# A branch for the middle expert: 64 or 128 places, chosen by its count of tokens

## The chip, the cores and the metric

The kernel runs on one core of a Trainium2 chip. The metric is the device time of one execution, in microseconds. A profiled execution also gives a trace: each instruction of the engines TensorE (PE, its weight loads PEld), VectorE (DVE), ScalarE (ACT) and GpSimd (POOL), and the DMA issues of SyncE (SP).

## What is computed

A diffusion block of two layers in float32 on 256 latent and 256 context tokens of width 1024. Layer 0 has differential attention and a SwiGLU network. Layer 1 has a recurrent mixer (RG-LRU) and, for the latent tokens, a mixture of eight experts, two for each token. The change lies in these experts, the last stage before the final norm:

```python
def swiglu(h, w_gate_up, w_down):
    gate, up = jnp.split(h @ w_gate_up, 2, axis=-1)
    return (jax.nn.silu(gate) * up) @ w_down

def moe_swiglu(h, router_w, w_gate_up, w_down):
    logits = (h @ router_w).astype(jnp.float32)
    top_val, top_idx = lax.top_k(logits, TOP_K)
    top_w = jax.nn.softmax(top_val, axis=-1)
    gates = ...
    for e in range(N_EXPERTS):
        y = y + gates[..., e:e + 1] * swiglu(h, w_gate_up[e], w_down[e])
    return y
```

An expert's inner width is 3584, so its weights are 1024 x 7168 and 3584 x 1024, and the eight together are 352 MB.

## The kernel before

Each expert computes only the tokens that chose it. They are gathered by a matmul with a one-hot matrix into columns, its "places", and scattered back the same way. Expert number 0 comes first; the other seven come in falling order of their counts of tokens, which the kernel finds itself (`by_counts`, L1643); SyncE then loads the seven experts' numbers into registers (`load_numbers`, L1915) and reads their weights from addresses made of them. An expert is "wide" (128 places) or "small" (64 places); `SMALL` (L46) makes the last three by count small, the other five wide. Should a count exceed the places, a test at the end (L1926 to L1928) runs the whole stage again for the tokens left over.

An expert's inner width is cut into seven chunks of 512. A chunk has a gate-up product (`gate_up`, L1727; four weight tiles), the activation, transposes of it (`act_T`, L1757) and a down product (`down`, L1776; two weight tiles), so six tiles of 1 MB. A tile is 128 x 2048 float32. A wide product needs its weights as two parts, high and low: ScalarE writes the high part (L135), VectorE the low one (L139), in halves of a tile, up to six halves ahead of the matmuls (`HL`), and each pair of weights and tokens takes three matmuls (L265 to L267), 48 for a gate-up product and 24 for a down one. A small product takes the tile as it is, in full float32: two matmuls of 64 columns stand beside each other in the array (L1738, L1784), and none of its weights are split.

A stream (`class stream`, L168) loads the tiles in the order of use into 13 places in SBUF. A place comes free when a wide tile's second half has been split, or when a small product has ended with it (`next_two`, L219); SyncE issues the next load then. `ORDER` (L46 to L56) sets the chunks' order: seven wide ones of expert 0, then seven groups of "small, wide, small, wide, small, wide, wide". `products` (L230) puts the down products behind: the down product of a small chunk comes just ahead of the next small gate-up, that of a wide chunk after the next wide gate-up.

Around a new expert, `experts` (L1704) works so: the one-hot matrix (`who`) is made after the gate-up product two chunks ahead; the gather's matmuls (`gather_mm`, L1310) come before the gate-up product of the chunk ahead, and the gathered tokens are scaled, shifted and split (`gather_split`, L1318) after it. In the middle of a wide gate-up product (`between`, L1891) stand the transposes and at most one scatter of an expert that is done. On the engines PE, DVE, ACT and POOL the order is as it is written; SyncE's is the framework's. The last chunk of all belongs to a wide expert: its end scatters, adds, squares, takes the root of the norm and writes the output (`scale_out`, L1806; `final_out`, L1698).

Of the kernel before, what the change touches and what calls it, by code (L numbers as in the profile page):

```python
# [45 lines left out]
SMALL = (5, 6, 7)  # L46
PLACES = tuple(64 if i in SMALL else P for i in range(NE))


_S = [(i, c) for i in SMALL for c in range(EC)]  # L50
_W = [(i, c) for i in range(NE) if i not in SMALL for c in range(EC)]
ORDER = _W[:EC]
for _n in range(EC):
    _s, _w = _S[3 * _n:3 * _n + 3], _W[EC + 4 * _n:EC + 4 * _n + 4]
    ORDER += [_s[0], _w[0], _s[1], _w[1], _s[2], _w[2], _w[3]]

# [32 lines left out]
def body(tc, nc, cst, rope, vec, lamv, modb, fing, x, ctx, w_m0, w_mod, w_q, w_k, w_v, w_o,  # L89
# [25 lines left out]

    def bank(name):
        return psp.tile([P, 512], F32, name=name, tag="b")
# [15 lines left out]
    def split_hi(h):  # L133
        h["hi"] = hip.tile([P, 1024], F32R, name="whi", tag="whi")
        A.copy(h["hi"][:, :h["w"]], h["src"])  # L135

    def split_lo(h, eng=V):
        h["lo"] = hip.tile([P, 1024], F32R, name="wlo", tag="wlo")
        eng.tensor_tensor(h["lo"][:, :h["w"]], h["src"], h["hi"][:, :h["w"]].bitcast(F32), op=OP.subtract)  # L139
# [18 lines left out]

    class part_of:
# [8 lines left out]
    class stream:  # L168
# [3 lines left out]
        def __init__(self, aps):  # L172
            self.aps, self.free, self.loaded, self.halves = aps, [], [], []
            self.n_split = self.n_used = self.n_tile = 0
            self.ahead, self.until = HL, len(aps)

# [53 lines left out]
    def products(order, small):  # L230
# [3 lines left out]
        for n, (i, c) in enumerate(order):  # L234
            s = i in small
            if s and pend[s]:
                yield "dn", *pend[s]
            yield "gu", i, c
            if not s and pend[s]:
                yield "dn", *pend[s]  # L240
            pend[s] = i, c
            if not s and pend[True] and not any(j in small for j, _ in order[n:]):
                yield "dn", *pend[True]
                pend[True] = None
        yield "dn", *pend[False]
# [1051 lines left out]
    def gather_banks(n, w=P):  # L1297

        per = KD // n
        banks = [bank("gath") for _ in range(n)]  # L1300
        return [(banks[k // per][:, k % per * w:(k % per + 1) * w], k % per, banks[k // per]) for k in range(KD)]
# [8 lines left out]
    def gather_mm(oh, small):  # L1310

        gps = gather_banks(1, 64) if small else gather_banks(2)
# [5 lines left out]
    def gather_split(eb, gps, scalar=(0, 1, 2, 3)):  # L1318

        hts = [eb.tile([P, 4, P], F32, name="ght", tag=tag) for tag in ("yh", "yl")]  # L1320
        xH = eb.tile([P, KD, P], F32R, name="xH", bufs=1)
        xL = eb.tile([P, KD, P], F32R, name="xL", bufs=1)

        def scaled(hb):
            for k in range(4 * hb, 4 * hb + 4):
                ht, g_, s_ = hts[hb][:, k % 4], gs2[:, k:k + 1], sh2[:, k:k + 1]
                if k in scalar:
                    A.activation(ht, gps[k][0], AF.Identity, scale=g_, bias=s_)  # L1328
                else:
                    V.tensor_scalar(ht, gps[k][0], g_, s_, op0=OP.mult, op1=OP.add)  # L1330

        scaled(0)
        if len(scalar) == 4 and scalar[3] == 3:
            scaled(1)
        for hb in range(2):
            ks = slice(4 * hb, 4 * hb + 4)
            A.copy(xH[:, ks], hts[hb])  # L1337
            V.tensor_sub(xL[:, ks], hts[hb], xH[:, ks].bitcast(F32))  # L1338
            if hb == 0 and scalar[3] != 3:
                scaled(1)  # L1340
        return xH, xL

    def gather_whole(eb, gps):

        ps = gps[0][2].rearrange("p (k n) -> p k n", k=KD)
        xF = eb.tile([P, KD, 64], F32, name="xF", bufs=1)
# [4 lines left out]
    with tc.manual_schedule(engines={ENG.PE, ENG.DVE, ENG.Activation, ENG.Pool, ENG.SP}):  # L1351
# [129 lines left out]
        first = stream(expert_tiles(ORDER, SMALL, numbers.__getitem__))  # L1481
        first.until = EC * 6 - 2
        first.add([rawp] * RAW)
# [6 lines left out]
        first.add(mrawL[:3])  # L1490
# [14 lines left out]
        first.add([part_of(mrawH[0][:, j]) for j in range(2)])  # L1505
        first.add(mrawL[3:])
# [12 lines left out]
        cnt = mo.tile([P, 1], I32, name="cnt")  # L1519
# [68 lines left out]
        first.add([part_of(mrawH[1][:, j]) for j in range(2)])  # L1588
# [26 lines left out]
        first.add(mrawR)  # L1615
        eb = pool(name="eb0", bufs=2)
# [5 lines left out]
        def gates_of_tokens():  # L1622

            scr = eb.tile([P, 74], F32, name="scr", tag="yh")
# [18 lines left out]
        def by_counts():  # L1643

            ck = bank("ck")
            mm(ck[:, 0:NE], ones, mask[:, 0], start=True, stop=False)
            mm(ck[:, 0:NE], ones, mask[:, 1], start=False, stop=True)
            scr = eb.tile([P, 3, NE * NE], F32, name="scr", tag="yl")
# [3 lines left out]
            V.tensor_copy(row[:, 0], ck[:, 0:NE])  # L1652
            V.tensor_add(row[:, 1], row[:, 0], lead)
# [15 lines left out]
            pick(row[:, 1], row[:, 0])  # L1669
            V.tensor_sub(row[:, 1], row[:, 1], places)  # L1670
# [3 lines left out]
            V.tensor_copy(cnt, cm)  # L1674
# [10 lines left out]
    def square(t, dh):  # L1685

        junk = bank("junk")
        A.activation(junk, XL[:, t, dh * 512:dh * 512 + 512], AF.Square, scale=D ** -0.5, accum_out=ssf[t][:, dh:dh + 1])
        if dh == 0:
            G.tensor_tensor(late["fo"][:, t, 0:512], XL[:, t, 0:512], late["fg"][:, 0:512], op=OP.mult)  # L1690
# [7 lines left out]
    def final_out(t):  # L1698
        rs, fo = ssf[t][:, 0:1], late["fo"][:, t]
# [4 lines left out]
    def experts(half, eb, E, tiles, order, small):  # L1704


        last, queue = order[-1][0], []

        def who(i, again=False):
            oh = eb.tile([P, 2, P], F32, name="ohp", bufs=1) if again else hp.tile([P, 2, P], F32, name="oh", tag="cr")  # L1710
            return one_hot(oh, key_at, i, i in small)

        def place(i):

            oh = E[i]["oh"]
            tp = bank("ohT")
            gp = bank("gateps")
# [3 lines left out]
            ohT = eb.tile([P, 2, P], F32R, name="ohTs", bufs=1) if i in small else hp.tile([P, 2, P], F32R, name="ohT", tag="SC")  # L1721
            A.copy(ohT.rearrange("p t n -> p (t n)"), tp[:, 0:2 * P])
            gs_ = eb.tile([P, 1], F32, name="gslot")
            V.tensor_copy(gs_, gp[:, 0:1])
            E[i].update(ohT=ohT, gate=gs_)

        def gate_up(i, c, between):  # L1727
            n = 256 if i in small else 512
            sg = None
            if i in small:  # L1730
                between()
                xF = E[i]["x"]
                gu = [bank("mg")]
# [299 lines left out]
```

## Time and profile before

| | us |
|---|---|
| median of three runs | 1746.3 (1746.25 to 1746.3) |
| profiled execution | 1744.36 |
| its span, first to last instruction | 1742.5 |
| TensorE busy in the span | 1689.8 |
| moved by DMA | 480.31 MB, 276 GB/s over the span |

The profile's page gives busy times of the engines over the span and in 40 slices; the trace behind it answers by line, by stretch of time, by waits, and by the chain of work that ended last. An L with a number is a line of the kernel before. The busy time of a group is the union of its instructions' times; matmuls overlap, so what one takes is read from the chain, in which each piece lasts until the next begins.

### The profile page before, as it was taken

To read this page: it belongs to the slowest core of one execution; us is meant where nothing else is said; L and a number is where in the kernel's file an instruction comes from. 1 tells how busy PE (TensorE), PEld (TensorE's weight loads), DVE (VectorE), ACT (ScalarE), POOL (GpSimd) and SP (SyncE) were. 2 spreads that over 40 slices of the span, in tenths; PEclk is the share of its full clock that TensorE was granted. 3 is DMA by queue.
4 is the path that set the end of the run, shared out by engine and by line. 5 is a ranking of instruction groups with operands and counts; after the bars stand their busy time and mean duration, and the time that the engine had idled before them with its cause. 6 is when DMAs were issued, how large, how long until landed. Compare 5 with 4: busy or idle time off the path is not lost. (4 is left out here: it accounts for less than half of the span.)

```text
span 1742.5 us, 21960 instructions
## 1 busy us (share of the span) xinstructions
PE 1689.8 (97%) x8060; PEld 1233.3 (71%) x8060; DVE 1205.9 (69%) x1694; ACT 885.6 (51%) x1289; POOL 63.4 (4%) x62
## 2 busy tenths in 40 slices
PE   8999999999999999987999999999999999999997
PEld 6877788887788877745786665666665766657564
DVE  5488878777757447897996775576664757648565
ACT  4367664322222216983875654454553645546353
POOL 0011100000000001131000000000000000000000
PEclk9999999999999999998999999999999999999998
DMA  9233323555656413356898899998999999999991
GB/s 375 103 145 146 146 97 118 203 200 193 231 190 238 136 70 121 112 224 241 312 392 308 329 421 405 420 371 355 397 402 420 370 421 391 372 383 411 386 422 50
DMA packets 75484, 480.31 MB, mean 276 GB/s; under 512 B 14284, under 2 KB 14924, under 8 KB 18920
## 3 DMA queue, kind: packets, MB, share of 16 engines
q1 hardware_dynamic: 66976, 474.38, 68.6%
q10 hardware_dynamic: 8392, 4.45, 1.0%
q8 instruction: 65, 1.06, 0.3%
q14 instruction: 51, 0.42, 0.1%
HBM read 477.70 MB, written 1.10 MB: 275 GB/s over the span
## 5 line engine op out<-in xcount | busy, mean ns | idle before, releaser
L139 DVE TENSOR_TENSOR wlo<-raw,whi 128x1024 fp32r<-128x1024 f32 x407 | 484.7, 1217 | 133.8 <-ACT whi L135 132.7
L135 ACT CAST whi<-raw 128x1024 fp32r<-128x1024 f32 x412 | 420.8, 1045 | 244.5 <-PE mg L266 80.2
L265 PE MATMUL mg<-whi,xH 128*128 128x512 f32 x560 | 228.3, 408 | 7.2 <-ACT xH L1337 7.2
L267 PE MATMUL mg<-wlo,xH 128*128 128x512 f32 x560 | 223.5, 399 | 2.0 <-DVE wlo L139 2.0
L266 PE MATMUL mg<-whi,xL 128*128 128x512 f32 x560 | 224.0, 400 | 0.9 <-DVE xL L1338 0.9
L139 DVE TENSOR_TENSOR wlo<-mraw,whi 128x1024 fp32r<-128x1024 f32 x124 | 148.3, 1222 | 35.6 <-ACT whi L135 35.3
L135 ACT CAST whi<-mraw 128x1024 fp32r<-128x1024 f32 x124 | 127.7, 1050 | 46.1 <-PE mg L266 40.6
L265 PE MATMUL gu<-hH,whi 128*128 128x512 f32 (+1 forms) x384 | 143.0, 372 | 0.0
L267 PE MATMUL gu<-hL,whi 128*128 128x512 f32 (+1 forms) x384 | 142.6, 371 | 0.0
L266 PE MATMUL gu<-hH,wlo 128*128 128x512 f32 (+1 forms) x384 | 142.6, 371 | 0.0
L265 PEld LDWEIGHTS mg<-whi,xH 128*128 128x128 f32 x560 | 106.6, 190 | 46.6 <-issue 13.6
L1738 PE MATMUL mg<-raw,xF 128*64 128x512 f32 x464 | 131.1, 594 | 0.0
L267 PEld LDWEIGHTS mg<-wlo,xH 128*128 128x128 f32 x560 | 106.5, 190 | 28.3 <-DVE wlo L139 2.4
L266 PEld LDWEIGHTS mg<-whi,xL 128*128 128x128 f32 x560 | 106.6, 190 | 25.9 <-DVE xL L1338 2.2
L1753 ACT ACTIVATE sges<-mg 128x256 f32<-128x256 f32 x21 | 8.1, 385 | 200.1 <-PE mg L1738 200.1
L265 PE MATMUL yp<-whi,aH 128*128 128x512 f32 x272 | 108.0, 397 | 0.0
L266 PE MATMUL yp<-whi,aL 128*128 128x512 f32 x272 | 107.4, 395 | 0.0
L267 PE MATMUL yp<-wlo,aH 128*128 128x512 f32 x272 | 107.3, 395 | 0.0
L1039 DVE SCALAR_TENSOR_TENSOR mac<-raw,SC,mac 128x512 f32<-128x512 f32 x140 | 98.2, 749 | 3.6 <-DMA raw<-w_mod 2.7
L1754 DVE TENSOR_TENSOR sges<-sges,mg 128x256 f32<-128x256 f32 x21 | 8.9, 422 | 125.4 <-ACT sges L1753 125.4
L1738 PEld LDWEIGHTS mg<-raw,xF 128*64 128x64 f32 x464 | 40.6, 137 | 62.0 <-issue 60.5
L265 PEld LDWEIGHTS gu<-hH,whi 128*128 128x128 f32 x384 | 72.3, 188 | 15.0 <-issue 2.5
(351 smaller groups left out, 3006.1 us busy)
## 6 DMA issues: line engine op xcount, KB each, us to landing
raw<-m_gu SPq DMA_DIRECT2D x158, 1024.0 KB
raw<-m_dn SPq DMA_DIRECT2D x75, 1024.0 KB
mraw<-m_gu SPq DMA_DIRECT2D x66, 1024.0 KB
raw<-w_mod SPq DMA_DIRECT2D x40, 1024.0 KB
mraw<-m_dn SPq DMA_DIRECT2D x37, 1024.0 KB
raw<-w_gu SPq DMA_DIRECT2D x22, 1024.0 KB
mw<-w_m SPq DMA_DIRECT2D x8, 1024.0 KB
raw<-w_dn SPq DMA_DIRECT2D x8, 1024.0 KB
```

What stands on the lines that cost most here:

```text
L135: A.copy(h["hi"][:, :h["w"]], h["src"])
L139: eng.tensor_tensor(h["lo"][:, :h["w"]], h["src"], h["hi"][:, :h["w"]].bitcast(F32), op=OP.subtract)
L265: mm(ps, lh, rh, start=start, stop=False)
L266: mm(ps, ll, rh, start=False, stop=False)
L267: mm(ps, lh, rl, start=False, stop=stop)
L1039: V.scalar_tensor_tensor(ac[:, q], w[:, j], SC[:, k, m:m + 1], ac[:, q], op0=OP.mult, op1=OP.add)
L1738: mm(gu[0][64 * h:64 * h + 64], xF[:, kk], w, start=(kk == 0), stop=(kk == KD - 1), tile_position=(0, 64 * h), skip_group_check=True)
L1753: A.activation(part, ps[:, 0:256], AF.Silu)
L1754: V.tensor_mul(part, part, ps[:, 256:512])
```

## The change

`FLEX = 4` names the expert that is fourth of the seven by count. `by_counts` also writes that expert's count into `cnt`. The stage runs as before up to the third chunk of expert 0 (`BEFORE = 3`); then all engines load the count, and a branch takes one of two bodies. Under 65 tokens, the fourth expert is small too: five wide chunks of expert 0 lead, then come 23 pairs "small, wide" and five small chunks. Otherwise the order is the old one. Each body goes on from copies (`fork`) of the state reached: stream, turns of the tiles, free banks, chunks under way. The loads before the branch are limited to the 28 tiles that both orders share.

So that both bodies can be written from one state, the stage's SBUF tiles and PSUM banks are no longer asked of pools: `ring` gives fixed tiles in turn, `banks` keeps a list of free banks, taken in front and given back behind. With two small chunks in a row, `products` puts the down product of the first behind the second's gate-up, and `between` stands in the middle of that gate-up. Where the new expert is of the other kind than the one before it, `gather` ends before the gate-up product that stands in between, and the one-hot is made in `between`, half a chunk or more earlier. A small expert can now be the last; its scatter goes to four banks. The test for left-over tokens at the end stays.

```diff
-SMALL = (5, 6, 7)
+FLEX = 4
+SMALL = tuple(range(FLEX + 1, NE))
...
+BEFORE = 3
...
+ORDERS = {False: (_mixed(SMALL, EC, "swswsww" * EC), SMALL)}
+ORDERS[True] = _mixed((FLEX,) + SMALL, EC - 2, "sw" * 23 + "s" * 5), (FLEX,) + SMALL
...
+        def fork(self, aps):
+
+            t = stream(aps)
+            t.free, t.loaded, t.halves = list(self.free), list(self.loaded), list(self.halves)
+            t.n_split, t.n_used, t.n_tile = self.n_split, self.n_used, self.n_tile
+            return t
...
-        first.until = EC * 6 - 2
+        first.until = (EC - 2) * 6 - 2
...
+            V.tensor_copy(cnt[:, 1:2], row[:, 1, FLEX:FLEX + 1])
...
             if ahead is not None:
                 gps = gather_mm(E[ahead]["oh"], ahead in small)
+                if (ahead in small) != (i in small):
+                    gather(ahead, gps)
...
                 if c == EC - 3:
                     E[i]["oh"] = who(i, True)
+                if n + 2 < len(order) and order[n + 2][1] == 0:
+                    j = order[n + 2][0]
+                    E[j] = {"oh": who(j)}
...
+                        for t in range(2 if i == last else 0):
+                            sp[t, dh] = pb.take()
+                            mm(sp[t, dh], E[i]["ohT"][rows, t].bitcast(F32), yg[rows], start=True, stop=True,
+                               tile_position=(64 * dh, 0))
...
+                    if last in small:
+                        act_T(*steps[order[-1]])
...
+    with manual():
+        state = experts(eb, E, first, *ORDERS[False], until=BEFORE, numbers_due=True)
...
+    def branch(flex):
+        with manual():
+            t = first.fork(expert_tiles(*ORDERS[flex], numbers.__getitem__))
+            t.load()
+            steps, queue, n, m = state
+            mem.update({k: v.fork() for k, v in before.items()})
+            experts(mem["eb"], {i: dict(e) for i, e in E.items()}, t, *ORDERS[flex], state=(dict(steps), list(queue), n, m))
+
+    fits = nc.values_load(cnt[0:1, 1:2], min_val=0, max_val=SEQ,
+                          skip_runtime_bounds_check_because="a count of at most 256 tokens")
+    with tc.If(fits < 65) as few:
+        branch(True)
+    with few.Else():
+        branch(False)
```

## Rows read from the trace of the kernel before

**Rows 1.** The page's busy times: engine, us, share of the span, instructions.

```profile
PE 1689.8 (97%) x8060; PEld 1233.3 (71%) x8060; DVE 1205.9 (69%) x1694; ACT 885.6 (51%) x1289; POOL 63.4 (4%) x62
```

**Rows 2.** Stretches: length, busy us by engine (instructions), granted clock, DMA share, GB/s.

```profile
900.00:1700.00 800.00, 785.43 (x3574) 519.51 (x3574) 518.93 (x577) 420.04 (x519) 0.00 (x0) 0.99 0.95 387
1000.00:1100.00 100.00, 100.00 (x454) 64.62 (x453) 64.48 (x70) 53.03 (x65) 0.00 (x0) 1.00 1.01 414
1060.00:1080.00 20.00, 20.00 (x96) 14.96 (x96) 16.08 (x21) 14.03 (x18) 0.00 (x0) 1.00 1.01 422
1300.00:1400.00 100.00, 97.88 (x445) 62.74 (x444) 61.65 (x72) 51.04 (x65) 0.00 (x0) 0.98 0.97 399
```

**Rows 3.** SyncE's waits before a load: releaser, us in total, times, longest.

```profile
SPq L122 <- DVE wlo L139: 691.6, 167, 20.0
SPq L122 <- PE yp L1784: 185.2, 20, 10.0
```

**Rows 4.** The chain that ended last, in order of time: start, us, work.

```profile
1669.38 3.58 PE yp L1784 x16
1672.96 6.87 PE mg L1738 x32
1679.83 0.44 PE mg L265
...
1685.63 0.65 PE aT L1761 x6
...
1697.48 3.58 PE yp L1784 x16
```

**Rows 5.** The page's DMA issues: tile, count, size of one.

```profile
raw<-m_gu SPq DMA_DIRECT2D x158, 1024.0 KB
```

**Rows 6.** TensorE's groups: busy us, mean ns, idle us before them and its releaser.

```profile
L265 PE MATMUL mg<-whi,xH 128*128 128x512 f32 x560 | 228.3, 408 | 7.2 <-ACT xH L1337 7.2
...
L1307 PE MATMUL gath<-oh,XN 128*128 128x128 f32 x160 | 19.0, 277 | 1.3 <-DVE oh L1284 1.3
...
L1307 PE MATMUL gath<-oh,XN 128*128 128x64 f32 x96 | 13.2, 304 | 2.4 <-DVE oh L1290 2.4
...
L1761 PE MATMUL aT<-cs,sges 128*128 128x128 f32 x42 | 8.1, 274 | 2.3 <-DVE aL L1773 2.3
```

**Rows 7.** Stretches as in rows 2, just after such waits.

```profile
955.00:960.00 5.00, 5.00 (x17) 3.94 (x16) 1.87 (x2) 2.39 (x3) 0.00 (x0) 0.68 1.01 426
1175.00:1180.00 5.00, 5.00 (x19) 4.42 (x19) 0.00 (x0) 0.21 (x1) 0.00 (x0) 0.50 1.01 428
1350.00:1355.00 5.00, 5.00 (x16) 3.94 (x15) 2.17 (x3) 2.10 (x3) 0.00 (x0) 0.66 1.01 421
1545.00:1550.00 5.00, 4.91 (x14) 3.87 (x15) 1.86 (x3) 1.77 (x2) 0.00 (x0) 0.66 1.01 421
```

**Rows 8.** The test at the end: ns min/median/max, first and last start.

```profile
L1926 PEldq TENSOR_LOAD <-cnt x1: 490/490/490, 1728.1 to 1728.1; - x1
...
L1926 ACTq TENSOR_LOAD <-cnt x1: 1059/1059/1059, 1734.3 to 1734.3; - x1
...
L1928 PEldq COMPARE_BRANCH  x1: 3370/3370/3370, 1728.7 to 1728.7; - x1
...
L1928 ACTq COMPARE_BRANCH  x1: 50/50/50, 1735.4 to 1735.4; - x1
...
L1928 ACTq EVENT_SEMAPHORE  x1: 17/17/17, 1739.4 to 1739.4; - x1
```

**Rows 9.** The end: a piece of the chain, and groups by line as in rows 6.

```profile
1727.24 2.84 PE scat L1853 x6
...
L1764 ACT COPY aF<-aT 128x256 f32<-128x256 f32 x21 | 7.9, 377 | 1.9 <-PE aT L1761 1.9
...
L1790 DVE SCALAR_TENSOR_TENSOR ygs<-yp,gslot,G2b 64x512 f32<-64x512 f32 x6 | 4.5, 750 | 6.6 <-PE yp L1784 6.6
...
L1841 PE MATMUL scat<-ygs,ohTs 64*128 64x512 f32 x24 | 9.0, 637 | 0.9 <-DVE ygs L1790 0.9
```

More of the change, by code (lines that the diff above doesn't have):

```diff
@@ L1480, in body, with places @@
         numbers = {0: 0}
-        first = stream(expert_tiles(ORDER, SMALL, numbers.__getitem__))
-        first.until = EC * 6 - 2
-        first.add([rawp] * RAW)
+        all_places = []
+        def places(pools):
+            new = [part_of(p.tile([P, 2048], F32, name="raw", tag="raw")) for p in pools]
+            all_places.extend(new)
+            return new
+        first = stream(expert_tiles(*ORDERS[False], numbers.__getitem__))
+        first.until = (EC - 2) * 6 - 2
+        first.add(places([rawp] * RAW))
         ws = {}
@@ L1504, in body @@
         mrawH = [hp.tile([P, 2, 2048], F32, name="mraw", tag="hH")]
-        first.add([part_of(mrawH[0][:, j]) for j in range(2)])
-        first.add(mrawL[3:])
+        first.add(places([part_of(mrawH[0][:, j]) for j in range(2)]))
+        first.add(places(mrawL[3:]))
+        halves = ring()
+        for tag in ("whi", "wlo"):
+            halves.put(tag, [hip.tile([P, 1024], F32R, name=tag, tag=tag) for _ in range(HL)])
+        mem["hi"] = halves
         for eng in (G, V, G):
@@ L1587, in body @@
         mrawH.append(hp.tile([P, 2, 2048], F32, name="mraw", tag="hL"))
-        first.add([part_of(mrawH[1][:, j]) for j in range(2)])
+        first.add(places([part_of(mrawH[1][:, j]) for j in range(2)]))
         close(lr2)
@@ L1702, in final_out, with experts @@
         nc.sync.dma_start(out[:, t], fo)
-    def experts(half, eb, E, tiles, order, small):
-        last, queue = order[-1][0], []
+    def experts(eb, E, tiles, order, small, state=None, until=None, numbers_due=False):
+        last, pb = order[-1][0], mem["ps"]
+        steps, queue, n, m0 = state or ({}, [], -1, 0)
         def who(i, again=False):
-            oh = eb.tile([P, 2, P], F32, name="ohp", bufs=1) if again else hp.tile([P, 2, P], F32, name="oh", tag="cr")
+            oh = eb.tile([P, 2, P], F32, name="ohp" if again else "oh")
             return one_hot(oh, key_at, i, i in small)
@@ L1730, in gate_up @@
             if i in small:
-                between()
+                run = order.index((i, c)) and order[order.index((i, c)) - 1][0] in small
+                if not run:
+                    between()
                 xF = E[i]["x"]
-                gu = [bank("mg")]
+                gu = [pb.take()]
                 for kh in range(2):
@@ L1739, in gate_up @@
                                tile_position=(0, 64 * h), skip_group_check=True)
+                    if run and kh == 0:
+                        between()
             else:
                 xH, xL = E[i]["x"]
-                gu = [bank(f"mg{h}") for h in range(2)]
+                gu = [pb.take() for h in range(2)]
                 for kh in range(2):
@@ L1863, in experts @@
             gather(0, gather_mm(E[0]["oh"], 0 in small))
-        todo, n, steps = list(products(order, small)), -1, {}
-        for m, (what, i, c) in enumerate(todo):
+        todo = list(products(order, small))
+        for m in range(m0, len(todo)):
+            what, i, c = todo[m]
+            if what == "gu" and n + 1 == until:
+                return steps, queue, n, m
             if what == "dn":
-                if m == len(todo) - 1 and half == 0:
-                    late["fg"] = mrawR[0].tile([P, D], F32, name="fg", tag="raw")
-                    late["fo"] = mrawR[1].tile([P, 2, D], F32, name="fo", tag="raw")
+                end = m == len(todo) - 1
+                if end:
+                    late["fg"], fo = [tiles.free.pop(0).tile() for _ in range(2)]
+                    late["fg"], late["fo"] = late["fg"][:, 0:D], [fo[:, t * D:(t + 1) * D] for t in range(2)]
                     nc.sync.dma_start(late["fg"], fing.to_broadcast([P, D]))
-                if m == len(todo) - 2:
+                    while queue:
+                        scatter(*queue.pop(0))
+                    if last in small:
+                        act_T(*steps[order[-1]])
+                if m == len(todo) - 2 and last not in small:
                     cur = steps[order[-1]]
```

223 lines of the change are left out of this document (143 added, 80 removed).

## The prediction, made before the change was run

> **What bounds the kernel now.** I read the page's busy times first: TensorE is busy 97% of the span, VectorE 69% [rows 1], so matmuls set the time unless a stage says otherwise. The stage of the change is the experts', about 800 to 1730 us, and it needs a table of its own, by stretches: over 900 to 1700 us TensorE is busy 785 of 800 us, VectorE 519, ScalarE 420, and the DMA engines' share is 0.95 at 387 GB/s [rows 2]. Two things are therefore nearly full, TensorE and the stream of weight tiles. To see which one holds the other, compare stretches: 1060 to 1080 us moves 422 GB/s at a share of 1.01, which I take for the stream's ceiling, while 1300 to 1400 us moves 399 with TensorE at 98% [rows 2]. The stream has holes where TensorE has none worth the name, and the longest waits of the issuing queue are for places that a product still holds (20 waits on the small `yp` products alone, 185.2 us) [rows 3]. So TensorE leads and the stream follows, some 8% below its ceiling (387 against 422).
>
> The chain that ended last then gives prices. A small chunk is its down product, 3.58 us, and its gate-up product, 6.87 us: 10.45 us. A wide chunk runs from 1679.83 to the next small product at 1697.48: 17.65 us, with 0.65 us of transposes of both kinds in it, so 17.0 us of its own [rows 4]. The reference, worked out on its inputs, gives the experts 110 tokens (number 0) and, sorted, 82, 70, 58, 56, 54, 52 and 30: the fourth of seven has 56, not over 64, so the branch with four small experts runs. The margin is 8 tokens.
>
> **The change part by part.**
>
> *One expert from wide to small.* Seven chunks at 17.0 - 10.45 = 6.55 us: -45.9 us. Its transposes go from four to two a chunk; six take 0.65 us [rows 4], so two take 0.22, and seven times that is -1.5 us. All of this lies on TensorE, which leads, so it is gained as long as the stream lets it be. Its 84 splits on ScalarE and VectorE go too and are priced at nothing: both have hundreds of idle microseconds in the stage [rows 2]. The bytes stay: each chunk still reads six tiles of 1024 KB [rows 5].
>
> *Gathers and one-hots come earlier.* Now, a new expert's gather is written out before the product of another expert and finished after it, so TensorE waits at the first product: 7.2 us on `xH`, 1.3 and 2.4 us on the one-hots ahead of the gathers, 2.3 us of a transpose behind VectorE [rows 6]. The new text finishes the gather before the other expert's product, which covers it (6.87 us against the short scale and split steps), and makes the one-hot half a chunk earlier. I take -10.9 us (7.2 + 1.3 + 2.4) and leave the 2.3 in; bounds 0 and -13.2. After such waits the granted clock is lower for a while: 0.68 in 955 to 960, 0.50, the 1.2 GHz level throughout, in 1175 to 1180, 0.66 in 1350 to 1355 and in 1545 to 1550 us [rows 7]. Lost there: 5 us times (0.32 + 0.50 + 0.34 + 0.34) = 7.5 us. Without the waits it should stay at 2.4 GHz: -7.5 us; bounds 0 and -7.5.
>
> *Entry of the branch.* Every engine loads the count and compares. The kernel before has one such test at its end, and there the load took 0.49 us on TensorE and 1.06 on ScalarE, and the compare-and-branch 3.37 us on TensorE [rows 8], where a large body was jumped over. Into the taken body the program runs on without a jump, so I take 0.49 + 0.1 = 0.6 us on TensorE; with a jump it would be 0.49 + 3.37 = 3.9 us; below nothing is excluded, since a load and a test are added. Behind it on TensorE wait the products of chunk 3. ScalarE and VectorE pay about 1.2 us each, covered by the six halves that are split ahead (six matmuls a half at 17.0 / 72 = 0.236 us: 8.5 us). SyncE enters when tile 28 has been issued, and what is queued behind its test are tile loads; 13 filled places (13 tiles at 1.049 MB / 422 GB/s = 2.5 us, 32 us) cover it. Without that cover it would be the same 0.6 to 3.9 us for each.
>
> *Exit of the branch.* The taken body ends with a jump over the other body. At the kernel's end today ScalarE's compare-and-branch starts at 1735.4 and its next instruction at 1739.4 [rows 8], 3.9 us after it, with nothing to wait for that the trace shows, and this lies on the end. The new kernel has two such jumps in a row: I take +3.9 us; bounds 0 (the second jump's target is near) and 4.5. The Trainium skill has a rule for this ("Runtime: NRT & Kernel Launch", Instruction fetch mechanics): a taken branch to a block that has not been prefetched waits for a fetch, straight code does not; by that rule, the trace agrees in the 3.37 us on TensorE, the entry is nearly free and each exit costs one fetch.
>
> *The end.* Today the last expert is wide: from its scatters at 1727.24 us to the end at 1742.5 it takes 15.3 us [rows 9]. After the change it is small: its last transposes stand between two products in the open (two matmuls, then a copy of 377 ns, with the signals about 0.9 us), and both scalings of the rows (750 ns each) stand before the first addition, where one does now [rows 9]. Four matmuls scatter it, 9.0 / 3 = 3.0 us an expert against 2.84 [rows 9], which is nothing. I take 0.9 + 0.7 = +1.6 us; bounds 0 and 3.
>
> *The stream.* From 900 us on the kernel before moved 800 us x 387 GB/s = 310 MB [rows 2], and the changed one must move the same. At 422 it needs 734 us and ends at 1634; the products would end at about 1727.2 - 65.8 + 0.6 = 1662. The stream thus has 28 us to spare, but in a pair of a small and a wide chunk alone it has none: 12 tiles take 30 us and the pair takes 28.1 [rows 4]. Only the gathers, one-hots and scatters between the experts give it time to catch up, and 13 places of slack pass it on. Bounds: 0 at 422, and at 399, the middling 100 us of today [rows 2], 310 MB takes 777 us, ends at 1677 and leaves one product (3.6 us), so +19 us. I take +5, near the lower end, since 1000 to 1100 us already ran at 414 with TensorE never idle [rows 2].
>
> Banks and tiles that take turns, and the count's extra copy, are given nothing: the waits they could add are for work that ended a chunk earlier.
>
> Sum: -45.9 - 1.5 - 10.9 - 7.5 + 0.6 + 3.9 + 1.6 + 5 = -54.7, so a span of 1742.5 - 54.7 = 1687.8 us. The profiled execution took 1744.4, 1.9 above its span, and the median of the runs is 1746.3, 3.8 above the span: 1691.6 us.
>
> **The rivals.**
>
> *The waits between experts stay.* The gather's steps run on ScalarE and VectorE in program order, and splits or scatters may stand ahead of them. For it: the waits' clock loss would stay too. Against it: both engines are idle through a small product. Time: 1691.6 + 18.4 = 1710.
>
> *The other body runs.* If the chip counts over 64 tokens, the tiles are as before: no gain of 47.4 us, a jump of 3.4 us at the entry, none at the exit. 1691.6 + 47.4 + 3.4 - 3.9 - 1.6 - 5 = 1732. Against it stands the margin of 8.
>
> *The stream takes over, and the kernel is slower.* A small product holds its two tiles until its matmuls end, a wide one frees them when they are split, ahead of use; the changed order has 28 small chunks for 21, alternating, so loads may start later and leave a hole each pair, and a starved TensorE may drop to 1.2 GHz besides. The last load is followed by a product, the end and its jump (3.6 + 0.9 + 0.7 + 15.3 + 3.9 = 24.4 us). It decides from the mean at which 310 MB end at 1742.5 - 24.4 = 1718, that is 310 / 818 = 379 GB/s, or a hole of (818 - 734) / 23 = 3.6 us a pair. At 370 it would be 1766 us. For it: today's mean is 387, and 185.2 us of waits are on small products [rows 3]. Against it: today's low mean comes from full places, not from late ones. The Trainium skill ("DMA: Bandwidth & Descriptors", Where 436 GB/s comes from) names about 358 GB/s as what the memory gives a core, which would make this rival certain; the trace disagrees with 422.
>
> **How the numbers follow.** Forecast 0.70: 1692. Waits stay 0.13: 1710. Other body 0.04: 1732. Stream, slower, 0.08: 1766. A milder stream that eats the whole gain, 0.03; the last 0.02 faster than the range. Low end: 1691.6 less the 5 of the stream, 3.9 of the exit, 1.6 of the end, 0.6 and the 2.3 us of the transpose is 1678, and chunk prices off by a tenth of a microsecond over 28 pairs make it 1675. High end: the forecast with the stream's upper bound (+14), or the waits staying with half of that, and a jump at the entry: 1720. A measurement of this kernel tells 0.2%, some 3.5 us, from no change. Faster 0.89, within 0.2% 0.03, slower 0.08.
>
> **What would show it.** TensorE's products on raw tiles should number 28 chunks for 21; a pair of chunks in the chain about 28.1 us; no idle time ahead of the first `mg` after a gather, and a granted clock of 1.00 there; the mean rate from 900 us on at or above 405 GB/s; one jump of 3.4 to 3.9 us more after the last output. The forecast is wrong if products wait on DMA in most pairs, if the chain turns to the stream, or if engines wait for one another at the branch's edges.

## The result, and the profile after

| | before | after |
|---|---|---|
| median, us | 1746.3 (1746.25 to 1746.55) | 1687.93 (1685.75 to 1688.58) |
| profiled execution, us | 1744.36 | 1685.75 |
| its span, us | 1742.5 | 1683.9 |

After to before is 0.9663, with a 95% interval of 0.9647 to 0.968: 58.4 us less by the medians and 58.6 by the spans, where -54.7 was forecast. The experiments below ran in three more sets, each with runs of the kernel before on its own chip (1741.0 to 1742.0 us there). So kernels are compared by their ratio to the kernel before of the same set, and a ratio is turned into microseconds with 1746.3. A ratio's interval is some 2.5 to 4.5 us to either side. The kernel before took 1744 to 1747 us at a granted clock of 0.986 to 0.988 over the span, as in the profiled execution (0.987), and 1740 to 1742 at 0.988 to 0.991, as in most executions of the later sets, one of 8133 us left out. So the gain is 58.4 us here and 55 in the set of e9, by its ratio of 0.9683.

A line L of this part is one of the changed kernel, which has one name, `b`, for all PSUM tiles. L332 to L334 are the wide products, L1829 and L1880 the small gate-up and down products, L1855 the transposes, L1374 the gather, L1954 the small scatter, L1887 its scaling, L1402 the high part of the gathered tokens, L2066 and L2068 the branch.

The page's busy times, which answer to [rows 1] (engine, us, share of the span, instructions):

```profile
PE 1636.5 (97%) x7878; PEld 1154.3 (69%) x7878; DVE 1100.8 (65%) x1595; ACT 794.3 (47%) x1194; POOL 61.3 (4%) x62
```

TensorE's share is 97% in both kernels. That number alone can't say what changed. Stretches can, with the columns of [rows 2] (length, busy us by engine with instructions, granted clock, DMA share, GB/s):

```profile
900.00:1650.00 750.00, 747.39 (x3442) 457.10 (x3442) 432.93 (x493) 344.99 (x440) 0.00 (x0) 1.00 1.00 412
900.00:1000.00 100.00, 100.00 (x464) 63.67 (x464) 60.44 (x68) 53.30 (x69) 0.00 (x0) 1.00 0.94 383
1000.00:1100.00 100.00, 100.00 (x467) 62.72 (x464) 60.27 (x69) 45.48 (x57) 0.00 (x0) 1.00 1.01 421
...
1650.00:1660.00 10.00, 10.00 (x50) 3.60 (x48) 3.11 (x5) 0.76 (x2) 0.00 (x0) 1.00 0.92 379
1660.00:1665.00 5.00, 4.48 (x24) 1.32 (x20) 0.00 (x0) 0.37 (x1) 0.00 (x0) 1.00 0.01 3
```

In 750 us TensorE sits idle for 2.6 us, and the granted clock is 1.00 (the 2.4 GHz level) over the whole stretch; before, 800 us held 14.6 idle ones and a clock of 0.99. The stream has come up beside it: a DMA share of 1.00, and from 1000 us on 421 GB/s. The two last rows show where it ends: 379 GB/s up to 1660, then 3. The last product of all begins at 1661.83. TensorE and the stream now finish the stage together.

The chain that ended last still runs along TensorE (start, us, work), a pair of chunks first, then the end:

```profile
1570.09 3.58 PE b L1880 x16
1573.67 6.87 PE b L1829 x32
1580.54 0.43 PE b L332
...
1586.33 0.66 PE b L1855 x6
...
1598.19 3.58 PE b L1880 x16
...
1661.41 0.38 ACT aF L1858
1661.83 3.70 PE b L1880 x16
1665.56 0.75 DVE ygs L1887
...
1673.59 0.75 DVE raw L1789
```

The pair takes 1598.19 - 1570.09 = 28.10 us, the 28.1 read from [rows 4]: no chunk became dearer or cheaper. The small gate-up products (L1829) number 896, 28 chunks of 32, where the kernel before had 672 (L1738), 21 chunks. At the end a copy (L1858) and the scaling (L1887) stand in the open, as foreseen for a small last expert.

TensorE's groups, as in [rows 6] (busy us, mean ns, idle us before them and its releaser):

```profile
L332 PE MATMUL b<-whi,xH 128*128 128x512 f32 x448 | 181.9, 406 | 1.2 <-ACT xH L1402 1.2
...
L1374 PE MATMUL b<-oh,XN 128*128 128x64 f32 x128 | 15.0, 276 | 0.0
...
L1374 PE MATMUL b<-oh,XN 128*128 128x128 f32 x96 | 11.5, 278 | 0.0
...
L1855 PE MATMUL b<-cs,sges 128*128 128x128 f32 x56 | 10.9, 276 | 0.0
...
L1954 PE MATMUL b<-ygs,ohTs 64*128 64x512 f32 x24 | 9.3, 637 | 2.6 <-DVE ygs L1887 2.6
```

Before, these groups waited 7.2, 2.4, 1.3, 2.3 and 0.9 us [rows 6, 9]. Three are at zero now. The 1.2 us left on `xH` are expert 0's own, at 826.72 us, ahead of any other product that could cover its gather. They are new: the kernel before waited 0.19 us there, at 818.09. The change also rewrites `gather_split`, which the lines shown of it leave out: it now scales the gathered tokens in their PSUM bank, one bank after the other. e7 below, with the old `gather_split`, waits 0.2 us on `xH` in all; that the rewriting makes the wait was not tested by itself. The last row is a new wait: three small scatters each wait 0.87 us for their scaling.

SyncE's longest waits before a load, over the whole execution, which answer to [rows 3] (releaser, us in total, times, longest):

```profile
SPq L135 <- DVE wlo L152: 561.9, 131, 20.0
SPq L135 <- PE b L1880: 217.4, 24, 9.9
```

Waits for a split fell from 691.6 us to 561.9; in the stage, from 830 us on, that is from 327.0 to 214.0. Two causes can meet in that, fewer tiles to split and loads that go out at the ceiling; they were not told apart. That the loader still has long waits on small products means little: they no longer leave the DMA engines empty.

The branch (duration in ns min/median/max, first and last start), which answers to [rows 8]:

```profile
L2066 PEldq TENSOR_LOAD <-cnt x1: 490/490/490, 866.0 to 866.0; - x1
...
L2068 PEldq COMPARE_BRANCH  x2: 86/1979/3872, 866.6 to 1667.2; - x2
L2068 ACTq COMPARE_BRANCH  x2: 38/39/40, 870.6 to 1673.6; - x2
...
L2075 ACTq COMPARE_BRANCH  x1: 55/55/55, 1677.5 to 1677.5; - x1
L2075 ACTq EVENT_SEMAPHORE  x1: 17/17/17, 1681.1 to 1681.1; - x1
```

L2068 stands there twice, once at the entry and once at the exit. On TensorE's sequencer the entry, into the body that follows, took 86 ns, and the exit, a jump over the other body, 3872. On ScalarE the exit starts at 1673.6 and the old test's at 1677.5, with a load of the count between; the next instruction after that test starts at 1681.1. Two jumps in a row, 3.9 and 3.6 us from one to the next.

### The profile page after: what moved, and what is told of

The parts are those of the page before. It is cut to its first block, busy times and chain, and to the rows that moved or that the text cites. A ratio compares the mean times of both kernels' runs of the same rounds, so it can differ in the third digit from the quotient of the medians.

```text
span 1683.9 us, 21275 instructions
## 1 busy us (share of the span) xinstructions
PE 1636.5 (97%) x7878; PEld 1154.3 (69%) x7878; DVE 1100.8 (65%) x1595; ACT 794.3 (47%) x1194; POOL 61.3 (4%) x62
## 4 chain that ended last, share of the span: by engine, by line
PE 91%; DVE 6%; ACT 1%; issue 1%; DMA 0%; POOL 0%; ACTq 0%; SPq 0%; POOLq 0%; DVEq 0%
PE b L1829 12%; PE b L332 9%; PE b L333 9%; PE b L334 9%; PE b L1880 6%; PE gu L332 5%; PE gu L333 5%; PE gu L334 5%; PE dacc L332 2%; PE dacc L333 2%; PE dacc L334 2%; PE b L1374 2%; PE p L334 1%; PE p L332 1%; PE p L333 1%; PE lg L1265 1%
## 5 line engine op out<-in xcount | busy, mean ns | idle before, releaser
L332 PE MATMUL b<-whi,xH 128*128 128x512 f32 x448 | 181.9, 406 | 1.2 <-ACT xH L1402 1.2
L1829 PE MATMUL b<-raw,xF 128*64 128x512 f32 x592 | 180.9, 594 | 0.0
L334 PE MATMUL b<-wlo,xH 128*128 128x512 f32 x448 | 177.6, 396 | 2.1 <-DVE wlo L152 2.1
L333 PE MATMUL b<-whi,xL 128*128 128x512 f32 x448 | 177.7, 397 | 0.0
L332 PE MATMUL gu<-hH,whi 128*128 128x512 f32 (+1 forms) x384 | 143.0, 372 | 0.0
L334 PE MATMUL gu<-hL,whi 128*128 128x512 f32 (+1 forms) x384 | 142.6, 371 | 0.0
L1829 PE MATMUL b<-mraw,xF 128*64 128x512 f32 x304 | 118.2, 595 | 0.0
L1829 PEld LDWEIGHTS b<-raw,xF 128*64 128x64 f32 x592 | 55.8, 137 | 87.4 <-issue 84.1
L332 PEld LDWEIGHTS b<-whi,xH 128*128 128x128 f32 x448 | 84.3, 188 | 36.1 <-issue 16.1
L334 PEld LDWEIGHTS b<-wlo,xH 128*128 128x128 f32 x448 | 84.3, 188 | 23.0 <-DVE wlo L152 2.6
L333 PEld LDWEIGHTS b<-whi,xL 128*128 128x128 f32 x448 | 84.4, 188 | 19.0 <-DVE xL L1403 0.5
L1880 PE MATMUL b<-raw,aF 128*64 128x512 f32 x352 | 91.2, 598 | 0.5 <-ACT aF L1858 0.5
L332 PE MATMUL b<-whi,aH 128*128 128x512 f32 x224 | 89.0, 397 | 0.0
L333 PE MATMUL b<-whi,aL 128*128 128x512 f32 x224 | 88.4, 395 | 0.0
```

The costliest lines, as they stand in the source:

```text
L332: mm(ps, lh, rh, start=start, stop=False)
L333: mm(ps, ll, rh, start=False, stop=False)
L334: mm(ps, lh, rl, start=False, stop=stop)
L1829: mm(gu[0][64 * h:64 * h + 64], xF[:, kk], w, start=(kk == 0), stop=(kk == KD - 1), tile_position=(0, 64 * h), skip_group_check=True)
L1880: mm(E[i]["y"][64 * dh:64 * dh + 64], lhs, w, start=(c == 0 and j == 0), stop=(c == EC - 1 and j == 3), tile_position=(0, 64 * dh), skip_g ...
```

## The experiments

| run | what it is | ratio to before | interval | median, us |
|---|---|---|---|---|
| e1_other_body | the old order's body runs | 0.9939 | 0.9917 to 0.996 | 1730.57 |
| e2_no_branch | the new order without a branch | 0.9655 | 0.9634 to 0.9675 | 1682.31 |
| e3_swapped | the bodies exchanged | 0.967 | 0.9651 to 0.969 | 1684.82 |
| e4_late_gather | gather and one-hot in their old places | 0.9797 | 0.9771 to 0.9823 | 1707.43 |
| e5_two_products | a third of the wide products left out | 0.9571 | 0.9555 to 0.9587 | 1665.49 |
| e6_five_small | five small experts | 0.9695 | 0.9679 to 0.9711 | 1688.48 |
| e7_before_early_gather | before, with the early gather alone | 0.9918 | 0.9901 to 0.9934 | 1726.69 |
| e8_eleven_places | two of the stream's places unused | 0.9721 | 0.9705 to 0.9737 | 1692.17 |
| e9_after_again | the changed kernel again | 0.9683 | 0.9669 to 0.9697 | 1687.21 |
| e12_no_branch_again | e2 again | 0.9657 | 0.9643 to 0.9671 | 1681.87 |
| e10_five_lead4 | five small, four wide chunks lead | 0.97 | 0.9685 to 0.9714 | 1689.17 |
| e11_four_lead4 | four small, four wide chunks lead | 0.974 | 0.9726 to 0.9755 | 1695.83 |

The theory: the gain is TensorE's, from one expert made small and from the early gathers, and the stream only keeps up. Its rivals are those of the prediction, and one that the trace of after suggests: that the stream is the bound now, so that the gain was cut short by it.

**Which body, and what the order is worth (e1).** The test is made one that 56 tokens fail, so the other body runs, with all the rest of the change in place.

```diff
-    with tc.If(fits < 65) as few:
+    with tc.If(fits < 1) as few:
```

> The changed kernel with the test set to 1 in place of 65, so that the other body runs: three small experts, old order, but with the early gathers and one-hots, the tiles that take turns and the branch. The prediction priced this as 1746.3 - 18.4 (waits and clock) + 0.6 + 3.4 (jump at the entry) = 1732 us. If the waits between experts were worth nothing, because the stream of tiles bounds the stage, it gives 1747 to 1750. If the tiles that take turns cost something, it lies above 1732 by that.

Measured: 0.9939, that is 1735.6 us, beside the 1732 that the prediction gave this rival; the interval, 3.7 us to either side, just reaches it. TensorE's group of products shows the old order (560 instructions; 448 in the other body):

```profile
L332 PE MATMUL b<-whi,xH 128*128 128x512 f32 x560 | 228.4, 408 | 3.0 <-ACT whi L148 1.8 <-ACT xH L1402 1.2
```

The changed kernel thus ran the new body, and the step from e1 to e9 is 0.9939 - 0.9683 = 2.56%, 44.7 us. The prediction's terms between these two kernels, -47.4 for the products, -3.4 of a jump at the entry, and +3.9, +1.6 and +5 for exit, end and stream, give -40.3. The 4.4 us more would fit the 5 of the stream, if they were not paid, but the two ratios' intervals (3.7 and 2.4 us) are as wide as that.

**What the early gathers are worth, from both sides (e4, e7).** e4 puts gather and one-hot back into their old places in the changed kernel:

```diff
-                if (ahead in small) != (i in small):
-                    gather(ahead, gps)
...
-                if n + 2 < len(order) and order[n + 2][1] == 0:
-                    j = order[n + 2][0]
-                    E[j] = {"oh": who(j)}
...
-            if ahead is not None and (ahead in small) == (i in small):
+            if ahead is not None:
                 gather(ahead, gps)
...
+            if n + 2 < len(order) and order[n + 2][1] == 0:
+                j = order[n + 2][0]
+                E[j] = {"oh": who(j)}
```

> The changed kernel with the gather's second part and the one-hots put back where the kernel before has them. If TensorE leads, as the prediction has it, the waits (10.9 us) and the lower clock behind them (7.5 us) come back in full: 1687.9 + 18 = 1706 us. If in the changed kernel the stream of tiles leads, the waits fall into time in which it catches up and cost a part of that: 1690 to 1698 us.

e7 makes the opposite edit, the same lines with plus and minus exchanged, in the kernel before, and nothing else:

> The kernel before with one part of the change: where the next expert is of the other kind, its gather ends ahead of the product in between, and the one-hot is made half a chunk earlier. Pools, banks and five wide experts stay, and there is no branch. If the waits and their lower clock are worth the 18.4 us of the prediction in the old order too: 1728. One gather of the four wide ones is of the same kind and keeps its place, so 1730 is as good. If the stream or the scaling's temporaries take it back: 1740 to 1746.

e4 measured 0.9797, against 0.9663 and 0.9683 for the changed kernel: 20 to 23 us lost, where 18.4 was forecast. Its groups and its stretch, columns as above:

```profile
L332 PE MATMUL b<-whi,xH 128*128 128x512 f32 x448 | 181.4, 405 | 9.7 <-ACT xH L1402 9.7
...
L1374 PE MATMUL b<-oh,XN 128*128 128x64 f32 x128 | 15.0, 276 | 3.5 <-DVE oh L1357 3.5
```

```profile
900.00:1650.00 750.00, 734.43 (x3350) 452.09 (x3350) 431.48 (x492) 343.93 (x436) 0.00 (x0) 0.99 0.97 401
```

The two named waits are back, 9.7 and 3.5 us for 1.2 and 0, the granted clock is 0.99 again, and the stream has slack once more (401 GB/s). e7 measured 0.9918: 14.3 us gained, 11.5 to 17.3 by the interval. Its groups (in that kernel L265 is the wide product and L1307 the gather) and its stretch:

```profile
L265 PE MATMUL mg<-whi,xH 128*128 128x512 f32 x560 | 226.5, 404 | 0.2 <-ACT xH L1337 0.2
...
L1307 PE MATMUL gath<-oh,XN 128*128 128x64 f32 x96 | 11.2, 275 | 0.0
```

```profile
900.00:1700.00 800.00, 796.80 (x3654) 527.58 (x3653) 531.02 (x592) 427.82 (x528) 0.00 (x0) 1.00 0.95 388
```

The waits are gone and the clock is at 1.00, with wide chunks as many as before. So the rival "the waits between experts stay" falls, and the size is about right: waits and clock together, 18.4 us forecast, 14.3 found in e7, whose interval ends at 17.3, and 20 to 23 in e4. In e4 the waits cost more than their own length: 13.0 us more of idle time in the stretch (busy 747.39 to 734.43) go with those 20 to 23. The clock behind them is a part of that: TensorE was granted 0.66 in e4 from 1125 to 1130 us, behind a wait of 0.96 us, though it kept 1.00 from 980 to 985, behind one of 2.84. In e7 11.4 us less of idle time (785.43 to 796.80) go with 14.3 in the end, too near to tell.

**What the branch costs (e2, e3, e12).** e2 and e12 write out only the new body, `branch(True)` in place of the load and the test. e3 puts it behind the `Else`, so that it is entered by a jump and left without one:

```diff
-    with tc.If(fits < 65) as few:
-        branch(True)
-    with few.Else():
-        branch(False)
+    with tc.If(fits > 64) as many:
+        branch(False)
+    with many.Else():
+        branch(True)
```

> The body with four small experts stands without test or branch; the left-over test at the end stays. The prediction gave the branch 0.6 us at the entry and 3.9 us at the exit: 1687.9 - 4.5 = 1683.4 us. The trace of the changed kernel shows the entry's test on TensorE's sequencer at 866 us while the matmuls run on without a gap, so exit alone: 1684. If the exit's jump hid behind the last output's transfer, no change: 1688.

> The two bodies change places: the test is for over 64 tokens, so the body with four small experts is now reached by a jump at the entry and runs on into the join without one. If the entry's jump (3.4 to 4.5 us on each sequencer) hides behind queued matmuls and halves split ahead, the exit's 3.6 us are saved: 1684 us. If TensorE stops for it, it gives back what the exit saves: 1688.

> The body with four small experts without test and branch, beside the changed kernel. The traces of both show the last output followed by 9.55 us with the branch and 6.12 us without, and no gap in the matmuls at the entry: 3.4 us less than the changed kernel. If something in the stage takes it back, less than 1 us.

> The changed kernel itself, as the measure of the three beside it on this chip: 0.966 to 0.967 of the kernel before, about 1684 to 1688 us.

Without a branch: 0.9655 and 0.9657; with it 0.9663 and 0.9683, so 1 to 5 us; the intervals touch. Within one set it is clearer: the five runs of e9 took 1685.76 to 1687.51 us, the five of e12 1681.38 to 1682.61. The traces are sharper. From the start of the last scaling of the output to the end of the span it takes 1683.9 - 1673.59 = 10.3 us with the branch and 1681.1 - 1674.21 = 6.9 in e2: the jump at the exit costs 3.4 us. The rest of what divides single traces arises before the branch: expert 0's `xH` releases TensorE at 826.72 and 828.52 us in two traces of the changed kernel, at 827.21 and 826.04 in two without a branch, with the same text up to there. That spread of 2.5 us is one of executions and builds, not of the branch.

In e3 the jump stands at the entry. TensorE's sequencer spent 4.89 us on it, and the products show this gap (timeline: start, us, work, idle time before it):

```profile
872.64 0.47 PE L332 MATMUL b<-whi,xH 128*128 128x512 f32 x1 [2.24 <-issue]
```

Only 2.24 of the 4.89 us reach the products: the sequencer is ahead of them and jumps while queued ones still run. In the changed kernel, where the body follows the test, no product is late at all (the load and the test stand at 866.0 and 866.6, and the products went on from 866 to 870 without a gap):

```profile
869.91 0.39 PE L334 MATMUL b<-wlo,aH 128*128 128x512 f32 x1
870.14 0.40 PE L332 MATMUL b<-whi,xH 128*128 128x512 f32 x1
```

So 2.24 us at the entry stand against 3.4 at the exit. The totals (0.967, against 0.9663 and 0.9683) can't tell the two ways of writing the branch apart. The traces can do more, if time is counted from the product that waits for expert 0's `xH` to the end of the span, since the spread of 2.5 us lies before it: 857.2 and 857.1 us in the changed kernel (its first trace and e9), 853.9 and 853.8 without a branch (e2 and e12), 854.5 with the bodies exchanged (e3, from 828.40 us). So the exchanged branch looks cheaper, by 1.2 us from the two jumps and by 2.6 in all; with a single trace of it that is not shown. The Trainium skill ("Runtime: NRT & Kernel Launch", Instruction fetch mechanics) says that a taken branch to a page not yet prefetched has to wait for a fetch; the 4.89 us of the taken entry beside 0.086 of the one that was not taken agree.

**Is the stream the bound now? (e5, e6, e8).** e5 leaves out part of the computation: of the three products of each wide pair, the one of the weights' low part with the tokens' high part. All loads and splits stay.

```diff
-                            mm3(gu[h], (xH[:, kk], xL[:, kk]), w, start=(kk == 0), stop=(kk == KD - 1))
+                            mm(gu[h], xH[:, kk], w[0], start=(kk == 0), stop=False)
+                            mm(gu[h], xL[:, kk], w[0], start=False, stop=(kk == KD - 1))
...
-                    mm3(E[i]["y"][dh], (aH[:, j * P:(j + 1) * P], aL[:, j * P:(j + 1) * P]), w,
-                        start=(c == 0 and j == 0), stop=(c == EC - 1 and j == 3))
+                    mm(E[i]["y"][dh], aH[:, j * P:(j + 1) * P], w[0], start=(c == 0 and j == 0), stop=False)
+                    mm(E[i]["y"][dh], aL[:, j * P:(j + 1) * P], w[0], start=False, stop=(c == EC - 1 and j == 3))
```

> The changed kernel without the third of the three matmuls of each wide product (the weights' low part times the tokens' high part is left out, so its output is a little less exact). All loads, splits and releases of tiles stay. A wide chunk's 17.0 us of matmuls become 11.3 us. If TensorE leads and the stream has the 28 us to spare of the prediction, the time falls by about 25 us, to the stream's floor at 422 GB/s: 1663 us. If the stream leads already in the changed kernel, it stays at 1683 to 1688 us.

It takes 28 wide chunks times 24 matmuls of 0.236 us, some 159 us, off TensorE. Measured: 0.9571, which is 1.12% or 19.6 us less than e9 (16 less by 0.9663). Its stretches, then its longest waits in the stage (who waited for whom, us, times, longest), then its chain:

```profile
900.00:1000.00 100.00, 98.58 (x456) 56.40 (x452) 65.87 (x76) 52.32 (x71) 0.00 (x0) 1.00 1.01 419
1000.00:1600.00 600.00, 523.05 (x2246) 302.93 (x2244) 344.14 (x399) 273.81 (x353) 0.00 (x0) 0.92 1.01 421
```

```profile
ACT whi L148 <- DMA mraw<-m_gu: 112.4, 25, 14.7
ACT whi L148 <- DMA raw<-m_gu: 103.4, 38, 14.7
```

```profile
1616.98 19.80 DMA raw<-m_dn
...
1636.82 3.65 PE b L1881 x14
```

The splits wait for tiles, the chain ends in the last tile, TensorE has 77 us of idle time in 600, its clock even falls to 0.92, and none of it matters: the stream runs at 419 to 421 GB/s from end to end. 159 us of work taken away are worth 16 to 20 us and no more. That is the room under TensorE before the stream is all there is.

e6 takes work off TensorE in the way the change does, by one more expert made small (the third of the seven by count, of 58 tokens), which is another -47 us by the prices of [rows 4]:

```diff
-FLEX = 4
+FLEX = 3
...
-ORDERS = {False: (_mixed(SMALL, EC, "swswsww" * EC), SMALL)}
-ORDERS[True] = _mixed((FLEX,) + SMALL, EC - 2, "sw" * 23 + "s" * 5), (FLEX,) + SMALL
+ORDERS = {False: (_mixed(SMALL, EC, "sw" * 21 + "s" * 7), SMALL)}
+ORDERS[True] = _mixed((FLEX,) + SMALL, EC - 2, "ssw" * 16 + "s" * 3), (FLEX,) + SMALL
```

> The branch for the third by count too (58 tokens): five small experts in the body that runs, order: five wide chunks, sixteen times small, small, wide, then three small. TensorE loses another 7 x 6.55 + 1.5 = 47 us of work, the stream nothing. If TensorE leads, time falls by up to the stream's 25 us, to 1663; if the stream leads, it stays within 5 us of 1688.

Measured: 0.9695, not faster than the changed kernel. Of 47 us nothing is left. Its stretches and its waits in the stage:

```profile
900.00:1000.00 100.00, 100.00 (x474) 56.88 (x474) 38.90 (x50) 34.69 (x49) 0.00 (x0) 1.00 0.93 383
1000.00:1600.00 600.00, 571.23 (x2579) 305.52 (x2578) 266.14 (x317) 205.35 (x272) 0.00 (x0) 0.98 1.01 420
```

```profile
ACT whi L148 <- DMA raw<-m_gu: 40.6, 31, 5.5
PE b L1880 <- ACT aF L1858: 18.5, 9, 4.0
ACT whi L148 <- DMA mraw<-m_gu: 15.1, 11, 6.1
```

From 1000 us on the stream is at 420 GB/s, so much of the gain went into waiting for it. Three things set it apart from e5, and none of them was tested by itself. From 900 to 1000 us the stream ran at 383 as in the changed kernel, where e5, with shorter wide products, had 419. On ScalarE, whose order is as written, a split that waits for its tile can stand ahead of a copy (L1858) that TensorE waits for: 18.5 us in nine waits. And the end is not the stream's: it was done by 1657 us, some 3 us earlier than in the changed kernel, but the last product began at 1665.74, against 1661.83, and TensorE's granted clock was 0.98 from 1000 to 1600 us and 0.50 from 1640 to 1645.

e8 leaves two of the 13 places unused, which changes no product:

```diff
-        first.add(places(mrawR))
+        places(mrawR)
```

> The changed kernel with two of the stream's 13 places left unused. If the stream has time to spare and the places pass it on, nothing changes: 1688 to 1690 us. If the stream ends together with the products, so that each hole counts, it takes 1692 to 1705 us.

Measured: 0.9721, 7 to 10 us slower than the changed kernel. The stretch ahead of the branch, first of e8, then of the changed kernel, and a late piece of e8's chain:

```profile
800.00:870.00 70.00, 66.35 (x310) 50.74 (x309) 56.14 (x108) 45.89 (x63) 1.10 (x2) 0.95 0.73 277
```

```profile
800.00:870.00 70.00, 66.34 (x316) 51.59 (x316) 56.12 (x109) 47.73 (x65) 1.10 (x2) 0.97 0.80 312
```

```profile
1644.76 17.08 DMA raw<-m_dn
```

Two tiles fewer are read before the pairs begin ((312 - 277) GB/s times 70 us = 2.45 MB, 5.8 us at 421 GB/s), and nothing makes up for them: near the end the chain turns to a tile. What the wide chunks at the front let the stream read ahead is used up by the end.

**A shorter lead (e10, e11).** If the lead of five wide chunks holds the stream at 383, four should let it rise sooner. e11 does so with four small experts, e10 with five; both have the bodies exchanged, and make the first one-hot at the branch's start. The order of e10 leaves out the down product of the last wide chunk, and with it that expert's scatter.

```diff
-ORDERS[True] = _mixed((FLEX,) + SMALL, EC - 2, "sw" * 23 + "s" * 5), (FLEX,) + SMALL
+ORDERS[True] = _mixed((FLEX,) + SMALL, EC - 3, "sw" * 24 + "s" * 4), (FLEX,) + SMALL
...
-        first.until = (EC - 2) * 6 - 2
+        first.until = (EC - 3) * 6 - 2
...
+        if state and order[n + 2][1] == 0:
+            j = order[n + 2][0]
+            E[j] = {"oh": who(j)}
```

> Five small experts, four wide chunks ahead of the first small one in place of five, bodies exchanged. With TensorE relieved, the stream runs at 420 GB/s from 1000 us on, and what is left are its holes in 800 to 1000 us, where wide chunks hold the places. One wide chunk less there frees 2 to 3 tiles' time: 5 to 8 us less than the changed kernel, if the stream alone sets the end. If the starved TensorE's lower clock or the new waits at the branch count, no gain or a loss of up to 5 us.

> The changed kernel with four wide chunks ahead in place of five and the bodies exchanged. The exchange gives 3.4 us at the exit and costs 2.2 us at the entry (both from traces); the shorter lead helps the stream but not TensorE, and its first gather follows the branch at once, 1 to 3 us. Sum: within 3 us of the changed kernel. If the stream were what bounds it: 3 to 6 us less.

Measured: 0.97 and 0.974, neither faster. The trace of e11 shows that the question was not put cleanly (timeline as above):

```profile
878.00 0.48 DVE L1357 TENSOR_SCALAR oh<-cs,key_at 128x128 f32<-128x128 f32 x2 [3.96 <-issue]
...
878.43 6.85 PE L1374 MATMUL b<-oh,XN 128*128 128x64 f32 x31 [8.41 <-DVE oh L1357]
```

The one-hot now stands behind VectorE's jump, and TensorE waits 8.41 us for it (8.44 in e10), more or less the 10 us by which e11 is slower than e9. The rate from 900 to 1000 us was 388 GB/s (387 in e10), hardly above 383. What a lead of four without that wait would bring stays open.

## Why the prediction was right, point by point

| term | forecast, us | found, us | from |
|---|---|---|---|
| products and transposes | -47.4 | -47 | a pair takes 28.10; e1 against e9 |
| waits between experts | -10.9 | -10.3 | 14.1 to 3.8 by the groups |
| clock after them | -7.5 | about -7 | granted 0.987 to 0.991 over the two spans |
| entry | +0.6 | 0 | no gap in the products |
| exit | +3.9 | +3.4 | after against e2 |
| the end | +1.6 | +1.5 | last product to last output |
| the stream | +5 | 0 | no tile in the chain of the stage |
| start of the stage | none | +0.6 | the counts, 851.53 to 853.10 us, less 1.0 that is among the waits |
| sum | -54.7 | about -59 | measured -58.6 by the spans |

- *TensorE leads, and the products' terms are gained whole.* Right. The prices of [rows 4] held to a hundredth of a microsecond a pair, which is why -47.4 could be trusted.
- *Waits and clock.* Right in size, and better in one item: the 2.3 us of the transposes, left in, went too. Against that stand 2.6 us of new waits on the scaling of small experts' rows, where the kernel before had 0.9 on that group; they were not foreseen. The dips of [rows 7] are gone: 0.68 and 0.50 became 1.00 in the same two stretches, 955 to 960 and 1175 to 1180 us. That waits and clock together cost about what was said is shown by e4 and e7; how they divide between the two was only read from the traces. Of the two, the clock is the weaker: 0.987 of 1742.5 us leaves 22.7 us ungranted, 0.991 of 1683.9 leaves 15.2, but in the set of e9 most runs of the kernel before were granted 0.990 and the changed kernel 0.989 to 0.990, so there the clock gave back next to nothing. Whether the change raises it in every execution is not shown.
- *Entry and exit.* Right: nothing and one jump. The prediction had the exit from ScalarE's one jump in [rows 8]; 3.4 us of it are new time.
- *The stream.* Here the prediction was right that the stream would not set the end, and in little else. The charge of +5 was not paid, and the working behind it was wrong: the stream was to end at 1634, 28 us ahead of the products. It ended at about 1660, some 2 us before the last product began. The step that failed is "at 422 it needs 734 us": between 900 and 1000 us the stream ran at 383, and only then at 421. In e5, whose wide products are a third shorter, it ran at 419 there, which points to products of the wide chunks that hold the places; whether it is the lead's length that decides, e11 leaves open. 310 MB at the mean of 412 take 752 us and end at 1652, not 1634; and there were 313 to move, 309 up to 1650 and 3.8 in the ten microseconds behind it, still at 379. That this cost nothing was luck of some 2 us, and e8 shows what lies on the other side of it. The reading of [rows 3] was off as well: the loader's longest waits there were not for products but for splits, 691.6 us in all and 327.0 in the stage, against 185.2.
- *The rival of the stream.* It was given 0.08 and a threshold of 379 GB/s for slower than before. The mean was 412. The Trainium skill ("DMA: Bandwidth & Descriptors", Where 436 GB/s comes from) puts the memory's limit at about 358 GB/s a core; here, where one core is at work, e5 measured 421 over 600 us, so the measurement decides. That small products hold their tiles did no harm: the loader's waits on them are long (217.4 us) while the DMA engines stay full.

The counts come 1.6 us later than before. 1.0 of that is expert 0's new wait on `xH`; what is left lies within the spread of 2.5 us that traces of the same text show there, so it is not shown to be the price of the extra count.

No other version here is shown to beat the changed kernel by itself; e3, the same with the bodies exchanged, may. Without a branch it is 1 to 5 us faster, but then the fourth expert has 64 places whatever its count.

## What to carry to other kernels

Before work is taken off the leading engine, work out how long the other one needs at its ceiling, and stretch by stretch, not with one rate: here -55 to -58 us were to be had, and the next step of the same kind (e6) brought nothing. Where a gather or another short side step stands between long products, write it out one product earlier; it was worth its waits at least (e7), and more than them in e4. Before you choose which body of a branch stands right behind the test, look where the jump falls: at the entry queued matmuls covered half of it (2.24 of 4.89 us were left), at the end nothing did (3.4).

## What was not expected of the hardware

- A jump over a large body took TensorE's sequencer 3.87 us (exit), 4.89 us (entry of e3) and 5.47 us (entry of e1), in which 2.24 and 1.78 us were missing from the products; a test that was not taken took 0.086 us.
- One core kept 421 GB/s for 600 us with tiles of 1 MB (e5), and 420 in e6.
- A starved TensorE fell to a granted clock of 0.92 in e5 without any loss of time, since the stream set the end.
